# Down projection of a decoder layer: 520 tokens divided into two moving parts, group by group

## The chip, the cores and the metric
The program runs on one NeuronCore of a Trainium2 chip (trn2). The metric is device time in microseconds, from launch to end, as the median of several executions. One further execution is taken with the hardware profiler; its views are what this document reads. TensorE (PE) does the matmuls and loads their weights (PEld), VectorE (DVE), ScalarE (ACT) and GpSimd (POOL) do the elementwise work, and SyncE (SP) issues all DMAs from one queue, in order.

## The reference
One decoder layer over 512 prompt tokens and 8 sample tokens, 520 in all, with a model width of 2048. A mixer (gated spatial heads beside a gated linear recurrence) is followed by a SwiGLU feed-forward net of width 5632, both with RMS norms before and after. What matters here is the end:

```
h = rms_norm(x, g_ffn_pre)
f = (silu(h @ w_gate) * (h @ w_up)) @ w_down
x = x + rms_norm(f, g_ffn_post)
```

`silu(h @ w_gate) * (h @ w_up)` are called the gated rows here: 5632 rows by 520 tokens, in 44 depth tiles of 128 rows.

## The kernel before
Activations lie transposed: features on the 128 partitions, tokens along the free dimension. The 520 tokens (`T`) are cut into two halves of 260 columns (`HT`, `cols(h)`). All large products are done in f32r, a 32-bit type with which a matmul needs one pass, and each operand is split into a high part (a cast to f32r) and a low part (the rest, by a subtraction). A product is the sum of three matmuls: high weights by high rows, high weights by low rows, low weights by high rows. In `product` these are lines 103 to 105; each has 128 x 128 weights as the stationary and 260 columns as the moving operand, and loads its own weights.

Weights come from DRAM as raw tiles of 128 x 1024 (tag `wr`, 3 buffers, line 74), are cast by ScalarE (`wh`, line 82, 4 buffers) and subtracted by VectorE (`wl`, line 84, 4 buffers). `pieces` keeps two pieces fetched beyond the ones in use.

Before the down projection, `seven` computes 40 of the 44 depth tiles of gated rows, in pairs, with seven block products for gate and up each (`term`, lines 736 to 738), and writes them to the DRAM tensor `fd` (line 795). The first four depth tiles were computed before (`gated`) and lie in `fd` too.

The down projection divides the 44 depth tiles into six groups, `CHUNKS = (4, 8, 8, 8, 8, 8)`. For one group the gated rows stand in SBUF as high and low halves: `load_f` reads one depth tile of 128 x 520 from `fd` into a `G` tile (line 789) and splits each half of 260 columns into its own pair of tiles of pool `ap` (`split`, lines 112 and 113; 64 buffers of 260 columns, the pool that also holds the rows of all earlier products). For each of the 16 output tiles `m`, `down` takes one piece of weights and computes the two halves one after the other, each with 3 matmuls per depth tile, 24 in a row (12 in the first group). The result is copied to the accumulator `Y[m]` in the first group (line 809) and added to it in the others (line 811). After every second output tile one depth tile of the next group is loaded and split.

The last group runs with the halves as the outer loop, and its weights are fetched twice. While the second half is computed, `finish_half(0)` normalises the first half, adds the residual rows `x1d` (line 829 loads them into tiles of `ap`, 16 per half) and writes it out (line 858). After the last matmul `finish_half(1)` does the same for the second half, with nine of the sixteen sums made by identity matmuls on TensorE (lines 839 and 851), the rest on VectorE (line 856), and the output of line 860.

Instructions are put in order by the scheduler of the kernel's framework: it takes what is ready in the order of the program, and where a tile has to be waited for, later instructions can be issued ahead of the one that waits. Each engine and the DMA queue then run their instructions strictly in the order so fixed.

The change touches the pools at the head of `trunk`, `load_f`, `down`, the loop that loads the first group, and the tiles of `finish_half`.

Of the kernel before, what the change touches and what calls it, by code (L numbers as in the profile page):

```python
# [7 lines left out]
F32 = mybir.dt.float32  # L8
F32R = mybir.dt.float32r
# [3 lines left out]
ALU = mybir.AluOpType  # L13
PSUM = bass.MemoryType.PSUM

P = 128
NP = 512
NS = 8
T = NP + NS
HT = T // 2  # L20
# [5 lines left out]
EPS = 1e-6  # L26
CHUNKS = (4, 8, 8, 8, 8, 8)
NSK = 4
LEVELS = (32, 8, 2)


@with_exitstack
def trunk(ctx: ExitStack, tc: tile.TileContext, a: dict):
    nc = tc.nc
    vec, act, pe, sp = nc.vector, nc.scalar, nc.tensor, nc.sync

    cp = ctx.enter_context(tc.tile_pool(name="cp", bufs=1))
    wp = ctx.enter_context(tc.tile_pool(name="wp", bufs=4, side="right"))
    ap_ = ctx.enter_context(tc.tile_pool(name="ap", bufs=64))
    phc = ExitStack()  # L40
    cc = phc.enter_context(tc.tile_pool(name="cc", bufs=16, side="right"))
    st = ctx.enter_context(tc.tile_pool(name="st", bufs=2))
    mm = ctx.enter_context(tc.tile_pool(name="mm", bufs=5, space=PSUM))
    ax = ctx.enter_context(tc.tile_pool(name="ax", bufs=3, space=PSUM))

    def const(name, dt=F32):
        t = cp.tile(list(a[name].shape), dt, name=name)
        sp.dma_start(t, a[name])
        return t

    def bank():
        return ax.tile([P, 512], F32, tag="ax", name="ax")

    def cols(h):
        return slice(h * HT, (h + 1) * HT)

    def part(pool, tag, bufs, dt=F32):

        return pool.tile([P, HT], dt, tag=tag, name=tag, bufs=bufs)

    def full(pool, tag, bufs=1, dt=F32):
        return pool.tile([P, T], dt, tag=tag, name=tag, bufs=bufs)
# [27 lines left out]
    def pieces(n, ahead=2):  # L90
        while queue and len(ready) < n + ahead:
            fetch()
        return [ready.pop(0) for _ in range(n)]

    def product(ws, xs, h, place=None):

        ps = place() if place else mm.tile([P, 512], F32, tag="mm", name="mm")
        n = len(xs)
        for k, x in enumerate(xs):
            wh, wl = ws[k // 8]  # L100
            xh, xl = x[h]
            c = slice((k % 8) * P, (k % 8) * P + P)
            pe.matmul(ps[:, :HT], lhsT=wh[:, c], rhs=xh, start=(k == 0), stop=False)  # L103
            pe.matmul(ps[:, :HT], lhsT=wh[:, c], rhs=xl, start=False, stop=False)  # L104
            pe.matmul(ps[:, :HT], lhsT=wl[:, c], rhs=xh, start=False, stop=(k == n - 1))  # L105
        return ps[:, :HT]

    def split(x, pool, tag, bufs, scale=None):
        hi = part(pool, tag, bufs, F32R)
        lo = part(pool, tag, bufs, F32R)  # L110
        if scale is None:
            act.copy(hi, x)
            vec.tensor_tensor(out=lo, in0=x, in1=hi.bitcast(F32), op=ALU.subtract)
        else:
            act.mul(hi, x, scale)
            vec.scalar_tensor_tensor(out=lo, in0=x, scalar=scale, in1=hi.bitcast(F32), op0=ALU.mult, op1=ALU.subtract)
        return hi, lo
# [43 lines left out]
    for i in range(KT):  # L161
# [3 lines left out]
        if i % 4 == 0:  # L165
            c = slice((i % 8) * P, (i % 8 + 4) * P)
# [19 lines left out]
    for k in range(KT):  # L186
        X.append([split(x0[k][:, cols(h)], ap_, "A", 64, g1[:, k:k + 1]) for h in range(2)])
        for m in range(2):
            if k % 8 == 0:
                W[m].append([wp.tile([P, 1024], F32R, tag=t, name=t) for t in ("wh", "wl")])  # L190
            hi, lo = W[m][-1]
            raw = w0[m][k // 8]
            if k % 4 == 0:
                for o, n in ((0, 1), (1, 3)) if k == 0 else ((k % 8, 4),):
                    c = slice(o * P, (o + n) * P)
                    act.copy(hi[:, c], raw[:, c])
                    vec.tensor_tensor(out=lo[:, c], in0=raw[:, c], in1=hi[:, c].bitcast(F32), op=ALU.subtract)
            c = slice((k % 8) * P, (k % 8 + 1) * P)
            for h in range(2):
                ps = first[2 * m + h][:, :HT]  # L200
# [16 lines left out]
    vec.memset(keep.rearrange("p (n t) -> p n t", t=32)[:, :, 0:1], 0.0)  # L217
    masks = {h: const(f"mask{h}", I32) for h in LEVELS[1:]}
    mone = const("mask1", I32)
# [18 lines left out]
    def step():  # L238
        for g in list(behind):
            if next(g, StopIteration) is StopIteration:  # L240
                behind.remove(g)

    ws = pieces(2)
# [303 lines left out]
    for h in range(8):  # L547
        w = {}
# [29 lines left out]
    for _ in range(2):  # L578
        for i in range(NSK):
            for nm in ("w_gate", "w_up"):  # L580
# [12 lines left out]
    fd = tc.dram_tile([FT, P, T], F32, name="fd")  # L593
# [30 lines left out]
    for h in range(2):  # L624
        for m in range(16):
            ps = product(pieces(2), OS, h)
# [29 lines left out]
    def combine():  # L656
        c0, c1 = cols(0), cols(1)
        for k in range(8):
            lo, hi = M[k], M[k + 8]
            vec.tensor_tensor(out=lo[:, c0], in0=lo[:, c1], in1=lo[:, c0], op=ALU.subtract)  # L660
            T1[k] = split(lo[:, c0], tp, "T", 48)
            nc.gpsimd.tensor_tensor(out=lo[:, c1], in0=hi[:, c1], in1=lo[:, c1], op=ALU.subtract)
            vec.tensor_tensor(out=hi[:, c1], in0=hi[:, c1], in1=lo[:, c0], op=ALU.subtract)
            T2[k] = split(hi[:, c1], tp, "T", 48)
            nc.gpsimd.tensor_tensor(out=hi[:, c0], in0=hi[:, c1], in1=hi[:, c0], op=ALU.subtract)
            T3[k] = split(lo[:, c1], tp, "T", 48)
            yield

    for i in range(NSK):
        g = product(pieces(2), X, 0)  # L670
# [8 lines left out]
    behind.append(combine())  # L679
    for i in range(NSK):  # L680
        g = product(pieces(2), X, 1)
        step()
        last = i == NSK - 1
        u = product(pieces(2, 0 if last else 2), X, 1)
# [12 lines left out]
    gp_ = ph4.enter_context(tc.tile_pool(name="gp", bufs=8, side="right", reuse_waits="tile"))  # L697
# [80 lines left out]

    for i in range(NSK, FT, 2):
        for nm in ("w_gate", "w_up"):  # L780
            queue.extend(quarters(a[nm], i, i == NSK and nm == "w_gate"))
    for n in (0, 1, 2, 3, 4, 5, 5):
        for m in range(16):
            want(a["w_down"][n - 1, m] if n else a["w_head"][m], 1024 if n else 512)
    F = []

    def load_f(i):
        f = full(gp_, "G", 8)
        sp.dma_start(f, fd[i])
        return [split(f[:, cols(h)], ap_, "A", 64) for h in range(2)]  # L790

    for i in range(NSK, FT, 2):
        gate = seven(None)
        for j, f in enumerate(seven(gate)):
            sp.dma_start(fd[i + j], f)
    for i in range(CHUNKS[0]):
        F.append(load_f(i))
    ph2.close()


    yp = ctx.enter_context(tc.tile_pool(name="yp", bufs=16, reuse_waits="tile"))
    Y = [None] * 16

    def down(ws, m, h, c):
        ps = product(ws, F, h)
        if Y[m] is None:
            Y[m] = full(yp, "Y", 16)
        if c == 0:
            act.copy(Y[m][:, cols(h)], ps)
        else:  # L810
            vec.tensor_tensor(out=Y[m][:, cols(h)], in0=ps, in1=Y[m][:, cols(h)], op=ALU.add)  # L811

    done = CHUNKS[0]
    for c in range(len(CHUNKS) - 1):
        G = []
        for m in range(16):
            ws = pieces(1)
            for h in range(2):
                down(ws, m, h, c)
            if m % 2:  # L820
                G.append(load_f(done))
                done += 1
        F = G

    def finish_half(h):
        xs = []
        for i in range(16):
            xs.append(part(ap_, "A", 64))
            sp.dma_start(xs[i], x1d[i, h])
        yield  # L830
        with tc.high_priority(4000):
            r = inv_rms(acc[h], D, load=False)

        sums = []

        def add(i):
            ps = bank() if i % 7 in (0, 3) else mm.tile([P, 512], F32, tag="mm", name="mm")
            sums.append(ps[:, :HT])
            pe.matmul(sums[i], lhsT=ident, rhs=xs[i], start=True, stop=False)

        for i in range(7 if h else 0):
            add(i)
        yield
        c = cols(h)
        for i in range(16):
            y = Y[i][:, c]

            o = Y[i & ~1][:, cols(i % 2)] if h else xs[i]
            vec.tensor_tensor(out=y, in0=y, in1=r, op=ALU.mult)
            if i < len(sums):  # L850
                pe.matmul(sums[i], lhsT=ident, rhs=y, start=False, stop=True)
                act.copy(o, sums[i])
                if i + 7 < 9:
                    add(i + 7)
            else:
                vec.tensor_tensor(out=o, in0=y, in1=xs[i], op=ALU.add)
            if h == 0:
                sp.dma_start(a["o_y"][i, h], o)
            elif i % 2:
                sp.dma_start(a["o_y"][i - 1:i + 1, h].rearrange("i p t -> p i t"), Y[i - 1].rearrange("p (i t) -> p i t", i=2))  # L860
            yield
# [4 lines left out]
    for h in range(2):  # L866
        next(ends[h])
        for m in range(16):
            down(pieces(1), m, h, 5)
            y = Y[m][:, cols(h)]  # L870
            add_square(acc[h], y, m == 0)
            act.mul(y, y, gf[:, m:m + 1])
            step()
        while behind:
            step()
        behind.append(ends[h])
# [5 lines left out]
def layouts(x_prompt, x_sample, state_hgrn, norm_mix_pre, norm_mix_post, w_in, ln_v_gain, ln_v_bias, spatial_w,  # L882
# [34 lines left out]
    arrays["ident"] = np.eye(P, dtype=np.float32)  # L917
    for hh in LEVELS[1:]:
        g = 32 // hh
# [38 lines left out]
```

## Time and profile before

| | |
|---|---|
| median of 2 runs | 2323.53 us (2323.21 to 2323.84) |
| profiled execution | 2318.88 us |
| its span, first to last instruction | 2317.2 us |
| mean granted TensorE clock | 0.993 |
| TensorE busy | 2266.3 us, 98% |
| VectorE busy | 1664.3 us, 72% |
| ScalarE busy | 1065.9 us, 46% |
| GpSimd busy | 220.6 us, 10% |
| DMA, mean rate | 134 GB/s |

All times in the views are microseconds from the start of the span, or nanoseconds where it says so. A matmul's duration in the trace includes the time it takes to pass through the array, during which the next one already runs; how fast matmuls follow one another is read from their starts, or from how many start in a stretch. The down projection lies between 1793 and 2300 us.

### The profile page before, as it was taken

The page shows a single profiled execution, that of the slowest core. Times are in us where ns is not written, and L with a number is a line of the kernel's source. Part 1 is how long each engine was busy: PE and PEld are TensorE (multiplying, and loading weights), DVE is VectorE, ACT ScalarE, POOL GpSimd, SP SyncE. Part 2 cuts the span into 40 slices and gives each one's busy share as a digit, 9 for nine tenths or more (in the row PEclk, how much of TensorE's full clock was granted, in tenths as well). Part 3 has the DMA queues.
Part 4 walks back from the last instruction along what each step waited for, and adds up shares of the span by engine and source line. Part 5 has one row for each costly group of instructions (what it writes and reads, how often), then busy time and mean ns, then how long its engine had stood idle before and what let it go on. Part 6 is the DMA issues. An engine that isn't in the chain of part 4 may idle for free.

```text
span 2317.2 us, 44793 instructions
## 1 busy us (share of the span) xinstructions
PE 2266.3 (98%) x18548; PEld 2256.2 (97%) x18548; DVE 1664.3 (72%) x2688; ACT 1065.9 (46%) x1607; POOL 220.6 (10%) x116
## 2 busy tenths in 40 slices
PE   8999999999999998999999999999999999999998
PEld 8999999999999998999999999999999999999998
DVE  8398777777555778888888888888888534434367
ACT  7286566666345555444343443444334512212155
POOL 0000000000000000322222222222221000000000
PEclk9999999999999999999999999999999999999999
DMA  6224333443335766543333333333333723332275
GB/s 224 92 88 125 113 114 111 120 120 120 115 110 182 214 209 194 176 158 115 115 110 126 119 115 124 119 120 110 118 119 102 229 92 129 112 113 95 90 240 156
DMA packets 130267, 310.16 MB, mean 134 GB/s; under 512 B 14928, under 2 KB 57360, under 8 KB 130064
## 3 DMA queue, kind: packets, MB, share of 16 engines
q1 hardware_dynamic: 130064, 307.30, 42.7%
q8 instruction: 145, 2.38, 0.4%
q14 instruction: 58, 0.48, 0.1%
HBM read 281.64 MB, written 25.61 MB: 133 GB/s over the span
## 4 chain that ended last, share of the span: by engine, by line
PE 80%; DVE 9%; DMA 8%; ACT 1%; issue 1%; SPq 0%; DVEq 0%; POOL 0%; ACTq 0%; POOLq 0%
PE mm L105 14%; PE mm L104 14%; PE mm L103 14%; PE mm L738 8%; PE mm L736 8%; PE mm L737 8%; DMA bc<-scr 5%; PE ax L738 3%; PE ax L736 3%; PE ax L737 3%; DVE wl L84 2%; PE ax L411 1%; DMA scr<-rows 1%; DMA wr<-w_up 1%; DVE S L483 1%
## 5 line engine op out<-in xcount | busy, mean ns | idle before, releaser
L105 PE MATMUL mm<-A,wl 128*128 128x260 f32 x3616 | 1026.2, 284 | 8.7 <-DVE wl L84 8.4
L103 PE MATMUL mm<-A,wh 128*128 128x260 f32 x3616 | 1031.3, 285 | 2.0 <-ACT wh L82 2.0
L104 PE MATMUL mm<-A,wh 128*128 128x260 f32 x3616 | 1026.0, 284 | 0.0
L82 ACT CAST wh<-wr 128x1024 fp32r<-128x1024 f32 (+1 forms) x460 | 475.4, 1035 | 771.6 <-PE mm L104 475.4
L84 DVE TENSOR_TENSOR wl<-wr,wh 128x1024 fp32r<-128x1024 f32 (+1 forms) x460 | 554.7, 1207 | 268.4 <-ACT wh L82 255.8
L105 PEld LDWEIGHTS mm<-A,wl 128*128 128x128 f32 x3616 | 685.0, 189 | 10.5 <-DVE wl L84 10.3
L103 PEld LDWEIGHTS mm<-A,wh 128*128 128x128 f32 x3616 | 684.8, 189 | 2.5 <-ACT wh L82 2.2
L104 PEld LDWEIGHTS mm<-A,wh 128*128 128x128 f32 x3616 | 685.0, 189 | 0.3
L738 PE MATMUL mm<-A,wl 128*128 128x260 f32 x960 | 271.1, 282 | 0.5 <-DVE wl L84 0.5
L737 PE MATMUL mm<-A,wh 128*128 128x260 f32 x960 | 270.8, 282 | 0.0
L736 PE MATMUL mm<-A,wh 128*128 128x260 f32 x960 | 270.4, 282 | 0.0
L82 ACT CAST wh<-ws 128x1024 fp32r<-128x1024 f32 x120 | 123.8, 1047 | 265.8 <-DVE ws L719 265.8
L811 DVE TENSOR_TENSOR Y<-mm,Y 128x260 f32<-128x260 f32 x160 | 68.4, 427 | 193.0 <-PE mm L105 192.8
L84 DVE TENSOR_TENSOR wl<-ws,wh 128x1024 fp32r<-128x1024 f32 x120 | 188.4, 1570 | 11.8 <-ACT wh L82 10.8
L736 PE MATMUL mm<-T,wh 128*128 128x260 f32 x640 | 181.4, 283 | 1.3 <-ACT wh L82 1.3
L738 PE MATMUL mm<-T,wl 128*128 128x260 f32 x640 | 180.8, 282 | 0.8 <-DVE wl L84 0.8
L738 PEld LDWEIGHTS mm<-A,wl 128*128 128x128 f32 x960 | 180.2, 188 | 0.7 <-DVE wl L84 0.7
L737 PEld LDWEIGHTS mm<-A,wh 128*128 128x128 f32 x960 | 180.8, 188 | 0.0
L736 PEld LDWEIGHTS mm<-A,wh 128*128 128x128 f32 x960 | 180.7, 188 | 0.0
L737 PE MATMUL mm<-T,wh 128*128 128x260 f32 x640 | 180.1, 281 | 0.0
L720 POOL TENSOR_TENSOR wr<-wr 128x1024 f32<-128x1024 f32 x40 | 95.8, 2396 | 478.5 <-DVE ws L717 478.5
L719 DVE TENSOR_TENSOR ws<-ws,wr 128x1024 f32<-128x1024 f32 x40 | 134.3, 3358 | 0.0
(229 smaller groups left out, 3123.2 us busy)
## 6 DMA issues: line engine op xcount, KB each, us to landing
wr<-w_gate SPq DMA_DIRECT2D x96, 512.0 KB, 4.0
wr<-w_up SPq DMA_DIRECT2D x96, 512.0 KB, 4.1
wr<-w_down SPq DMA_DIRECT2D x96, 512.0 KB, 3.6
wr<-w_in SPq DMA_DIRECT2D x92, 512.0 KB, 4.1
wr<-w_out SPq DMA_DIRECT2D x64, 512.0 KB, 3.8
bc<-scr SPq DMA_DIRECT2D x32, 384.0 KB, 5.3
G<-fd SPq DMA_DIRECT2D x44, 260.0 KB, 3.9
fd<-G SPq DMA_DIRECT2D x40, 260.0 KB, 3.6
```

The costliest lines, as they stand in the source:

```text
L82: act.copy(hi[:, :n], raw[:, :n])
L84: vec.tensor_tensor(out=lo[:, :n], in0=raw[:, :n], in1=hi[:, :n].bitcast(F32), op=ALU.subtract)
L103: pe.matmul(ps[:, :HT], lhsT=wh[:, c], rhs=xh, start=(k == 0), stop=False)
L104: pe.matmul(ps[:, :HT], lhsT=wh[:, c], rhs=xl, start=False, stop=False)
L105: pe.matmul(ps[:, :HT], lhsT=wl[:, c], rhs=xh, start=False, stop=(k == n - 1))
L411: pe.matmul(pl[:, c * 192:(c + 1) * 192], lhsT=kk[:, cg * P:(cg + 1) * P], rhs=qq[:, cg], start=True, stop=True)
L719: vec.tensor_tensor(out=s2, in0=s1, in1=raws["11"], op=ALU.subtract)
L720: nc.gpsimd.tensor_tensor(out=raws["21"], in0=raws["11"], in1=raws["21"], op=ALU.subtract)
L736: pe.matmul(ps, lhsT=wh[:, c], rhs=xh, start=(start and k == 0), stop=False, skip_group_check=not start)
L737: pe.matmul(ps, lhsT=wh[:, c], rhs=xl, start=False, stop=False, skip_group_check=not start)
L738: pe.matmul(ps, lhsT=wl[:, c], rhs=xh, start=False, stop=(k == len(xs) - 1), skip_group_check=not start)
L811: vec.tensor_tensor(out=Y[m][:, cols(h)], in0=ps, in1=Y[m][:, cols(h)], op=ALU.add)
```

## The change
A list `CUTS` gives each group its own division of the 520 tokens: in the six groups the first part has 260, 256, 260, 512, 384 and 260 columns, and the second part the other 260, 264, 260, 8, 136 and 260. `load_f` makes one high and one low tile of 544 columns (2176 bytes) per depth tile, in a pool `fp` of 32 buffers, with one cast and one subtraction over all 520 columns; the parts are slices of these tiles. In the third group the second half is put 12 columns further on, so that it begins at byte 1088 of its tile; elsewhere the second part follows directly on the first. `down` holds the three matmuls itself. The pool `ap` is closed before the down projection, and the residual rows of `finish_half` take tiles of `fp`. The number of matmuls, the weights and their order stay.

```diff
+CUTS = ((260, False), (256, False), (260, True), (512, False), (384, False), (260, False))
...
-    ap_ = ctx.enter_context(tc.tile_pool(name="ap", bufs=64))
+    st = ctx.enter_context(tc.tile_pool(name="st", bufs=2))
+    pha = ExitStack()
+    ap_ = pha.enter_context(tc.tile_pool(name="ap", bufs=64))
...
-    def load_f(i):
-        f = full(gp_, "G", 8)
-        sp.dma_start(f, fd[i])
-        return [split(f[:, cols(h)], ap_, "A", 64) for h in range(2)]
...
-    for i in range(CHUNKS[0]):
-        F.append(load_f(i))
     ph2.close()
+    pha.close()
+    fp = ctx.enter_context(tc.tile_pool(name="fp", bufs=32, reuse_waits="tile"))
...
+    def load_f(i, c):
+        cut, gap = CUTS[c]
+        f = full(gp_, "G", 8)
+        sp.dma_start(f, fd[i])
+        hi, lo = (fp.tile([P, T + 24], F32R, tag="F", name="F", bufs=32) for _ in range(2))
+        if gap:
+            def two(t):
+                return t[:, :T + 24].rearrange("p (h t) -> p h t", h=2)[:, :, :HT]
+            f2 = f.rearrange("p (h t) -> p h t", h=2)
+            act.copy(two(hi), f2)
+            vec.tensor_tensor(out=two(lo), in0=f2, in1=two(hi).bitcast(F32), op=ALU.subtract)
+            return [(hi[:, o:o + HT], lo[:, o:o + HT]) for o in (0, HT + 12)]
+        act.copy(hi[:, :T], f)
+        vec.tensor_tensor(out=lo[:, :T], in0=f, in1=hi[:, :T].bitcast(F32), op=ALU.subtract)
+        return [(hi[:, x], lo[:, x]) for x in (slice(0, cut), slice(cut, T))]
+
     def down(ws, m, h, c):
-        ps = product(ws, F, h)
+        cut, gap = CUTS[c]
+        x = (slice(0, cut), slice(cut, T))[h]
+        (wh, wl), = ws
+        ps = mm.tile([P, 512], F32, tag="mm", name="mm")[:, :x.stop - x.start]
+        for k, f in enumerate(F):
+            fh, fl = f[h]
+            w = slice(k * P, k * P + P)
+            pe.matmul(ps, lhsT=wh[:, w], rhs=fh, start=(k == 0), stop=False)
+            pe.matmul(ps, lhsT=wh[:, w], rhs=fl, start=False, stop=False)
+            pe.matmul(ps, lhsT=wl[:, w], rhs=fh, start=False, stop=(k == len(F) - 1))
         if Y[m] is None:
             Y[m] = full(yp, "Y", 16)
         if c == 0:
-            act.copy(Y[m][:, cols(h)], ps)
+            act.copy(Y[m][:, x], ps)
         else:
-            vec.tensor_tensor(out=Y[m][:, cols(h)], in0=ps, in1=Y[m][:, cols(h)], op=ALU.add)
+            vec.tensor_tensor(out=Y[m][:, x], in0=ps, in1=Y[m][:, x], op=ALU.add)
+    for i in range(CHUNKS[0]):
+        F.append(load_f(i, 0))
...
-                G.append(load_f(done))
+                G.append(load_f(done, c + 1))
...
-            xs.append(part(ap_, "A", 64))
+            xs.append(part(fp, "F", 32))
```

## Rows read from the trace of the kernel before

**Rows 1.** The page's head, busy shares and chain that ended last.
```profile
PE 2266.3 (98%) x18548; PEld 2256.2 (97%) x18548; DVE 1664.3 (72%) x2688; ACT 1065.9 (46%) x1607; POOL 220.6 (10%) x116
PE 80%; DVE 9%; DMA 8%; ACT 1%; issue 1%; SPq 0%; DVEq 0%; POOL 0%; ACTq 0%; POOLq 0%
```

**Rows 2.** Stretches of the down projection: busy time (instructions) by engine, clock, DMA.
```profile
1932.00:2022.00 90.00, 90.00 (x757) 90.00 (x756) 37.15 (x61) 21.59 (x32) 0.00 (x0) 1.00 0.35 111
2024.00:2114.00 90.00, 90.00 (x752) 90.00 (x751) 36.63 (x59) 21.21 (x32) 0.00 (x0) 1.00 0.36 110
2208.00:2300.00 92.00, 92.00 (x769) 91.74 (x768) 69.53 (x126) 56.95 (x93) 0.00 (x0) 1.00 0.68 212
```

**Rows 3.** A stretch at half clock, then TensorE's order of time around it.
```profile
439.90:443.20 3.30, 2.74 (x13) 2.77 (x14) 3.30 (x7) 2.00 (x4) 0.00 (x0) 0.50 0.34 100
...
440.46 1.09 PE L437 MATMUL ax<-ident,kh 128*128 128x128 f32 x4 [2.65 <-DVE kh L357]
...
441.77 0.42 PE L105 MATMUL mm<-A,wl 128*128 128x260 f32 x1
441.99 0.42 PE L103 MATMUL mm<-A,wh 128*128 128x260 f32 x1
```

**Rows 4.** Order of time in the first group: matmuls and weight loads.
```profile
1800.07 0.19 PEld L103 LDWEIGHTS mm<-A,wh 128*128 128x128 f32 x1
1800.19 0.29 PE L103 MATMUL mm<-A,wh 128*128 128x260 f32 x1
1800.19 0.19 PEld L104 LDWEIGHTS mm<-A,wh 128*128 128x128 f32 x1
```

**Rows 5.** Order of time: f32 matmuls of 128 columns, four and two in a row.
```profile
186.55 0.61 PE L518 MATMUL ax<-A,ibt 128*128 128x128 f32 x4
...
186.99 0.39 PE L520 MATMUL ax<-qh,Sc 128*128 128x128 f32 x2
```

**Rows 6.** f32 matmuls of 192 columns: eight in a row, and their group's mean.
```profile
143.78 1.46 PE L411 MATMUL ax<-qx,kx 128*128 128x192 f32 x8
...
L411 PE MATMUL ax<-qx,kx 128*128 128x192 f32 x192 | 36.0, 329 | 0.0
```

**Rows 7.** Groups by line (busy us, mean ns): splits of 260 columns, and operations of 520.
```profile
L112 ACT CAST A<-G 128x260 fp32r<-128x260 f32 x88 | 29.9, 407 | 3.3 <-DMA G<-fd 3.2
L113 DVE TENSOR_TENSOR A<-G,A 128x260 fp32r<-128x260 f32 x88 | 32.5, 422 | 3.2 <-ACT A L112 3.0
L774 ACT ACTIVATE G<-G 128x520 f32<-128x520 f32 x20 | 12.8, 640 | 7.3 <-DVE G L772 7.3
L179 DVE TENSOR_TENSOR C<-C 128x520 f32<-128x520 f32 x15 | 10.5, 702 | 0.7
```

**Rows 8.** Order of time at the stage's start: ScalarE, then VectorE.
```profile
1794.55 1.53 ACT L112 CAST A<-G 128x260 fp32r<-128x260 f32 x4 [0.37 <-DMA G<-fd]
...
1795.61 1.44 DVE L113 TENSOR_TENSOR A<-G,A 128x260 fp32r<-128x260 f32 x4
```

**Rows 9.** SP's order of time at the end, its waits, landings.
```profile
2230.65 0.38 SPq L829 DMA_DIRECT2D A<-x1d  x1
2262.55 0.82 SPq L858 DMA_DIRECT2D o_y<-A  x2
2283.66 8.49 SPq L858 DMA_DIRECT2D o_y<-A  x5
...
SPq L477 <- DMA o_ss<-S: 34.8, 18, 3.7
...
A<-x1d SPq DMA_DIRECT2D x32, 130.0 KB, 3.5
o_y<-A SPq DMA_DIRECT2D x16, 130.0 KB, 4.5
```

**Rows 10.** Order of time at the end: first and last use of the rows.
```profile
2300.18 1.92 PE L839 MATMUL mm<-A,ident 128*128 128x260 f32 x8
2312.92 0.43 DVE L856 TENSOR_TENSOR Y<-Y,A 128x260 f32<-128x260 f32 x1
```

More of the change, by code (lines that the diff above doesn't have):

```diff
@@ L38, in trunk @@
     wp = ctx.enter_context(tc.tile_pool(name="wp", bufs=4, side="right"))
-    ap_ = ctx.enter_context(tc.tile_pool(name="ap", bufs=64))
+    st = ctx.enter_context(tc.tile_pool(name="st", bufs=2))
+    pha = ExitStack()
+    ap_ = pha.enter_context(tc.tile_pool(name="ap", bufs=64))
     phc = ExitStack()
     cc = phc.enter_context(tc.tile_pool(name="cc", bufs=16, side="right"))
-    st = ctx.enter_context(tc.tile_pool(name="st", bufs=2))
     mm = ctx.enter_context(tc.tile_pool(name="mm", bufs=5, space=PSUM))
```

## The prediction
> **What bounds the kernel now.** I read the page from its top: the busy shares, then the chain of work that ended last [rows 1]. TensorE is busy for 98% of the span and the chain lies on it for 80%. I cut the time of the down projection into stretches, each inside one group of depth tiles; three of them stand here [rows 2]. In all of them TensorE is busy for the whole stretch at full clock, while VectorE is busy for some 40% and ScalarE for 24%, more only in the last one, where the norms and outputs come in. So this stage is bound by how often a matmul can start: 752 in 90 us are 119.7 ns from start to start, 757 are 118.9, and I use 120. The 260 columns of one matmul would take 108.3 ns at 2.4 GHz; where the clock stands at half (1.2 GHz) they start 0.22 us apart, which is 260/1.2 = 217 ns with nothing added [rows 3]. At full clock there are thus 11.7 ns more than the columns explain.
>
> The order of time inside the stage [rows 4] shows what else each matmul needs: a weight load of its own. The load for the next matmul starts when the present one starts, and the next one follows 0.12 us later. That a load is never earlier is the row on which this prediction hangs. How fast loads can follow each other when the columns are few is seen at the f32 matmuls of 128 columns [rows 5]: four in 0.61 us, two in 0.39, so (0.61 - 0.39)/2 = 110 ns apart, and I take 111. (An f32 matmul runs two cycles a column, 107 ns here, so the load alone could be shorter; that is rival (a).)
>
> **The change, part by part.** Each group keeps its number of matmuls: 16 output tiles by 8 depth tiles by 3 products by 2 parts, which is 384 pairs (192 in the first group, with 4 depth tiles). A pair now costs 240 ns. Only the columns of the two halves of a pair change, and `down` runs all 24 matmuls of one part before the other, so a short part cannot hide its loads behind a long one.
>
> Fourth group, 512 and 8. The long one: 512/2.4 = 213.3 ns, plus the 11.7 of the 260 as a fixed addition, 225. Ends: 215, if almost nothing is added (the f32 matmuls of 192 columns [rows 6] take 0.329 us each and eight of them 1.46, so they start (1.46 - 0.33)/7 = 161 ns apart, little over the 160 of two cycles a column), and 236, if the addition grows with the columns (120 x 512/260). The short one streams 8 columns in 3 ns but loads 128 columns of weights: 111, ends 109 and 120 (what a load and matmul take today). Sum 336 (324 to 356), 96 more per pair, and 384 x 96 = **36.9 us** (32 to 45). No row has loads closer together than that, so I take the load as the bound. The Trainium skill ("TensorE: Matmul & The Clock Gate", section "Back-to-back issue gap") speaks against this: N/2.4 + 2.5 ns, with a floor of some 60 cycles. By it the pair would be 215.8 + 25 = 241 ns and the group would cost nothing; this stands below as a rival.
>
> Fifth group, 384 and 136. 160 + 11.7 = 172 (162 to 177), and for 136, whose columns need only 57 ns, again the load, 111 (109 to 120): 283 (271 to 297), 43 more, 384 x 43 = **16.4 us** (12 to 22).
>
> Second group, 256 and 264: 118.4 + 121.7 = 240 with the fixed addition, the same in proportion: **0**. If 256 falls to the load's 111 it is 384 x -7 = -3 us.
>
> First, third and last group, 260 and 260. The second half now begins 1040 bytes into its tile, in the third group 1088. No row shows a half that shares a tile. The stretches of [rows 2] differ by 0.8 ns though their tiles lie at other places; half of that for 1,920 matmuls is 1 us either way, and I take **0**.
>
> The split of the gated rows. Per tile two casts and two subtractions of 260 columns (407 and 422 ns) become one of each with 520, which cost about what the 520-column operations of the trace cost, 640 and 702 [rows 7]. That saves some 0.3 us a tile on both engines, under cover of TensorE: a tile is loaded per two output tiles, at least 2 x 24 x 120 ns = 5.8 us apart. The cover is missing only at the start of the stage. There the casts of the third and fourth tile begin at 1794.55 and their subtractions run to 1797, with matmuls already waiting for them tile by tile [rows 8]; both halves must now be split before the first part can use them: 2 x (702 - 422) + (640 - 407) = 0.8 us. The tile memory is no later: the new tiles lie over those that the last but one `term` of `seven` frees. I take **1 us**; ends 0 (the wait falls into slack) and 4 (all four tiles are split after that stage's last matmul: 4 x 0.70 + 0.64, and the DMA behind).
>
> The end. `finish_half` took its residual rows from 64 half tiles, both halves early: the last of the 32 loads is issued at 2231, before the first output of line 858 at 2262 [rows 9]. Now 32 full tiles hold the last group's 16 and the first half's 16 rows, so each row of the second half must wait until the output DMA of a first-half row has left its tile; those outputs go out between 2262 and 2292. SP issues in order, and behind such a wait stand the weight loads of the last group, for which the casts and then TensorE wait. The same pattern, a DMA into a tile that a DMA must leave, is there at line 477: 34.8 us in 18 waits, 1.9 each, at most 3.7. Sixteen of them are 31 us within the last 38 us of matmuls, beside 27 weight and output issues of 0.33: SP is nearly full, but weights are fetched two to three pieces ahead and one piece lasts 24 x 120 ns = 2.9 us. The last rows would land around 2292 + 4.5 + 3.5 = 2300, and they are first used at 2300 to 2313 [rows 10]. I take **2 us**, ends 0 and 10 (half of what 16 waits of 3.7 would exceed the 38 us by). A gain is excluded: nothing is taken off the path there.
>
> Sum: 36.9 + 16.4 + 0 + 0 + 1 + 2 = **56 us** (low 32 + 12 - 3 - 1 = 40, high 45 + 22 + 1 + 4 + 10 = 82). The profiled execution took 2318.9 us for a span of 2317.2, and so 2375 with the change; the median of the runs, 2323.5, lies 4.6 above it, so I forecast 2380 (2364 to 2405).
>
> **Rivals.**
> (a) *Columns alone set the pace.* If loads are pulled further ahead when matmuls are short, a pair costs 520 columns however they are divided: 120/260 x 520 = 240 ns in every group, and only the 3 us of the split and the end are left, 2327: no change. It decides if 8-column matmuls start much closer than 109 ns. For it speaks that the 260 columns are not bound by the load alone, which could go at 110; against it that in no row does a load start before the preceding matmul has started. By the skill's gap rule named above, 256 and 384 would even gain (222 ns for each of these pairs), and the time would be about 2313.
> (b) *The clock falls in the fourth group.* Each run of 24 short matmuls lasts 24 x 111 = 2.7 us and streams 192 columns in it. With a wait of TensorE of 2.65 us, the clock came to stand at half from 439.9 to 443.2 [rows 3]. If TensorE counts as idle in such a run, each fall costs a stretch of 3.3 us in which 260 columns take 0.217 instead of 0.12, so about 1.5 us; with 16 runs, 24 us: 2404. If the clock stays down for the group, a pair costs 427 + 222, 313 more, and it is 2500. Against it: the loads go on throughout.
> (c) *Few columns lose the fast f32r rate.* All f32r matmuls of the trace have 260 columns. The f32 ones of 192 columns stand in the trace as two records of 161 ns [rows 6], 1.68 ns a column. If 136 columns run so, they take 229 instead of 111, 384 x 118 = 45 us more: 2425; if 8 columns too load their weights twice, another 43: 2468. The trace neither shows nor excludes it.
> (d) *The end of the kernel* is SP's: if each of the 16 waits lasts the 4.5 us of such an output's median landing [rows 9], they are 72 us, 34 more than the 38: 2380 - 2 + 34 = 2412.
>
> **How the numbers follow.** Forecast 0.48, (a) 0.12, (b) 0.17, (c) 0.17, (d) 0.04, and 0.02 for a gain that I cannot place. The predicted time is the forecast's, 2380. The range leaves out (a), the worse half of (c) and the rare end of (b): 2358 to 2435. The 2% that a measurement of this kernel can tell from no change are 46 us, a bound at 2370. All of (b), (c), (d) lie above it, and of the forecast's 2364 to 2405 about five parts in six: slower 0.78. Within 2%: (a) and the rest of the forecast, 0.20. Faster by over 2% would need all 4,224 matmuls 11 ns shorter, which no row suggests: 0.02.
>
> **What would show it.** In the profile after, matmuls of 8 and of 136 columns start 109 to 120 ns apart, those of 512 and 384 some 225 and 172; the fourth group lasts about 129 us, the fifth 109, the others 92 (46 for the first). Starts at 4 to 60 ns prove (a), half clock in the fourth group (b), 200 ns and more at 136 columns (c), and idle TensorE in the last 46 us behind SP (d). The forecast is wrong if the short parts come cheaper than a load, or if the columns over 260 cost more than in proportion.

## The result and the profile after

The changed kernel takes 2402.35 us (median of 2 runs, 2398.49 to 2406.21) against 2323.53: ratio 1.034, 95% interval 1.027 to 1.041. It is slower by 79 us, where 57 were forecast as the likeliest and 35 to 112 as the range. Its profiled execution took 2406.21 us for a span of 2404.5, 87.3 more than the span before.

Where these 87.3 us lie is read by cutting the down projection at the first matmul of each group, in both traces (us from the first start of a group to the first of the next; group 6 ends at the first matmul of the sums behind it):

| stretch | before | after | more | forecast |
|---|---|---|---|---|
| up to the last matmul of `seven` | 1793.0 | 1799.4 | 6.4 | 0 |
| from there to the stage's first matmul | 0.1 | 1.4 | 1.3 | 1 |
| group 1, 260 and 260 | 46.5 | 46.6 | 0.1 | 0 |
| group 2, 256 and 264 | 92.1 | 92.4 | 0.3 | 0 |
| group 3, 260 and 260 with the gap | 91.6 | 92.5 | 0.9 | 0 |
| group 4, 512 and 8 | 92.2 | 149.2 | **57.0** | 36.9 |
| group 5, 384 and 136 | 92.3 | 111.7 | **19.4** | 16.4 |
| group 6, 260 and 260 | 92.4 | 93.9 | 1.5 | 2 with the end |
| from that matmul to the end | 17.0 | 17.4 | 0.4 | |

The first row is not the change: it varies by 16 us between executions of kernels that are the same up to there (the last section). Without it the table gives 81 us, close to the 79 of the medians.

The stretches of groups 2, 4, 5 and 6 in the changed kernel, to be held against [rows 2]; columns as there, the first of the last three is TensorE's granted clock:

```profile
1848.00:1938.00 90.00, 90.00 (x751) 90.00 (x750) 34.48 (x51) 18.32 (x21) 0.00 (x0) 1.00 0.34 108
2032.20:2181.40 149.20, 149.20 (x770) 127.55 (x768) 36.65 (x54) 19.18 (x21) 0.00 (x0) 0.87 0.23 71
2181.50:2293.10 111.60, 111.60 (x769) 111.60 (x769) 38.09 (x56) 21.81 (x24) 0.00 (x0) 0.98 0.26 78
2293.20:2387.00 93.80, 93.80 (x772) 93.59 (x772) 69.99 (x126) 57.14 (x93) 0.00 (x0) 1.00 0.72 212
```

TensorE is busy throughout, as before, and the same 768 matmuls stand in each of the last three stretches. What changed is how far apart they start, and in the fourth group the clock: 0.87 on average. The clock's own record has twelve stretches of 3.41 us at half behind that group's sixteen runs of short matmuls, against none in the same groups before. Eleven lie in group 4; the twelfth begins 0.9 us into group 5, behind the last run.

One turn from short to long matmuls in that group, in order of time:

```profile
2058.27 0.25 PE L827 MATMUL mm<-F,wh 128*128 128x8 f32 x1
2058.38 0.25 PE L828 MATMUL mm<-F,wl 128*128 128x8 f32 x1
2058.49 0.47 PE L826 MATMUL mm<-F,wh 128*128 128x512 f32 x1
2058.80 0.39 PE L827 MATMUL mm<-F,wh 128*128 128x512 f32 x1
2059.03 0.40 PE L828 MATMUL mm<-F,wl 128*128 128x512 f32 x1
2059.27 0.41 PE L826 MATMUL mm<-F,wh 128*128 128x512 f32 x1
2059.50 0.60 PE L827 MATMUL mm<-F,wh 128*128 128x512 f32 x1
2059.90 0.63 PE L828 MATMUL mm<-F,wl 128*128 128x512 f32 x1
2060.32 0.63 PE L826 MATMUL mm<-F,wh 128*128 128x512 f32 x1
...
2062.88 0.42 PE L826 MATMUL mm<-F,wh 128*128 128x512 f32 x1
2063.14 0.40 PE L827 MATMUL mm<-F,wh 128*128 128x512 f32 x1
2063.38 0.40 PE L828 MATMUL mm<-F,wl 128*128 128x512 f32 x1
```

Matmuls of 8 columns start 0.11 us apart: the weight load, as forecast. Those of 512 start 0.23 apart until 2059.50 (the first of a run 0.31), then some 0.43, and from 2062.88 on 0.23 to 0.26 again. The median at half clock, 427 ns, is 512/1.2: the clock is at half for 3.4 us, right behind a run of short matmuls. The two stretches at the two levels of the clock:

```profile
2059.50:2062.90 3.40, 3.40 (x10) 2.62 (x9) 1.23 (x1) 0.11 (x1) 0.00 (x0) 0.50 0.29 52
2062.90:2065.60 2.70, 2.70 (x13) 2.21 (x12) 0.00 (x0) 0.00 (x0) 0.00 (x0) 0.99 0.32 129
```

Rival (b) thus stands beside the forecast, not in its place. The price in group 4: eleven times 3.41 us in which a 512-column matmul takes 427 ns instead of 234, so 11 x 3.41 x (1 - 234/427) = 17.0 us. In group 5 the twelfth makes matmuls of 384 columns take 320 ns instead of 175: 3.41 x (1 - 175/320) = 1.5 us. Together they are 18.5 us. Four of the sixteen runs have no fall behind them; no run shows why.

### The profile page after: what moved, and what is told of

Its sections match the earlier page's. It is cut to its first block, busy times and chain, and to the rows that moved or that the text cites. A ratio compares the mean times of both kernels' runs of the same rounds, so it can differ in the third digit from the quotient of the medians.

```text
span 2404.5 us, 44695 instructions
## 1 busy us (share of the span) xinstructions
PE 2345.1 (98%) x18548; PEld 2313.1 (96%) x18548; DVE 1661.6 (69%) x2644; ACT 1061.7 (44%) x1563; POOL 221.3 (9%) x116
## 4 chain that ended last, share of the span: by engine, by line
PE 82%; DMA 8%; DVE 7%; ACT 1%; issue 1%; SPq 0%; DVEq 0%; POOL 0%; ACTq 0%; POOLq 0%
PE mm L828 8%; PE mm L826 8%; PE mm L827 8%; PE mm L739 8%; PE mm L741 8%; PE mm L740 8%; PE mm L107 7%; PE mm L106 7%; PE mm L108 7%; DMA bc<-scr 5%; PE ax L740 3%; PE ax L739 3%; PE ax L741 3%; DVE wl L87 1%; PE ax L414 1%
## 5 line engine op out<-in xcount | busy, mean ns | idle before, releaser
L108 PE MATMUL mm<-A,wl 128*128 128x260 f32 x2208 | 630.3, 286 | 9.6 <-DVE wl L87 9.5
L106 PE MATMUL mm<-A,wh 128*128 128x260 f32 x2208 | 637.5, 289 | 2.0 <-ACT wh L85 1.9
L107 PE MATMUL mm<-A,wh 128*128 128x260 f32 x2208 | 631.0, 286 | 0.0
L108 PEld LDWEIGHTS mm<-A,wl 128*128 128x128 f32 x2208 | 422.5, 191 | 11.3 <-DVE wl L87 11.1
L106 PEld LDWEIGHTS mm<-A,wh 128*128 128x128 f32 x2208 | 424.3, 192 | 2.8 <-ACT wh L85 2.4
L107 PEld LDWEIGHTS mm<-A,wh 128*128 128x128 f32 x2208 | 423.1, 192 | 0.2
L826 PE MATMUL mm<-F,wh 128*128 128x260 f32 (+6 forms) x1408 | 422.0, 300 | 1.1 <-ACT F L814 1.1
L827 PE MATMUL mm<-F,wh 128*128 128x260 f32 (+6 forms) x1408 | 422.3, 300 | 0.0
L828 PE MATMUL mm<-F,wl 128*128 128x260 f32 (+6 forms) x1408 | 422.0, 300 | 0.0
L826 PEld LDWEIGHTS mm<-F,wh 128*128 128x128 f32 x1408 | 270.3, 192 | 8.6 <-ACT F L814 1.3
L827 PEld LDWEIGHTS mm<-F,wh 128*128 128x128 f32 x1408 | 270.9, 192 | 7.3
L828 PEld LDWEIGHTS mm<-F,wl 128*128 128x128 f32 x1408 | 270.6, 192 | 7.3
L741 PE MATMUL mm<-A,wl 128*128 128x260 f32 x960 | 270.2, 282 | 0.4 <-DVE wl L87 0.4
L740 PE MATMUL mm<-A,wh 128*128 128x260 f32 x960 | 270.5, 282 | 0.0
L739 PE MATMUL mm<-A,wh 128*128 128x260 f32 x960 | 270.5, 282 | 0.0
L834 DVE TENSOR_TENSOR Y<-mm,Y 128x260 f32<-128x260 f32 (+6 forms) x160 | 68.5, 428 | 263.6 <-PE mm L828 263.6
L739 PE MATMUL mm<-T,wh 128*128 128x260 f32 x640 | 181.4, 283 | 1.6 <-ACT wh L85 1.6
```

The source lines that it names most:

```text
L739: pe.matmul(ps, lhsT=wh[:, c], rhs=xh, start=(start and k == 0), stop=False, skip_group_check=not start)
L740: pe.matmul(ps, lhsT=wh[:, c], rhs=xl, start=False, stop=False, skip_group_check=not start)
L741: pe.matmul(ps, lhsT=wl[:, c], rhs=xh, start=False, stop=(k == len(xs) - 1), skip_group_check=not start)
L826: pe.matmul(ps, lhsT=wh[:, w], rhs=fh, start=(k == 0), stop=False)
L827: pe.matmul(ps, lhsT=wh[:, w], rhs=fl, start=False, stop=False)
L828: pe.matmul(ps, lhsT=wl[:, w], rhs=fh, start=False, stop=(k == len(F) - 1))
```

## The experiments

The theory: a matmul costs the longer of its weight load (111 ns for 128 columns of weights) and its columns, and a run of 24 matmuls with hardly any columns makes the clock fall. The rivals: matmuls of 512 columns are slow in themselves; short f32r matmuls run at the f32 rate; the split, the pools and SP at the end cost more than the division. All kernels below are the changed kernel with other entries in `CUTS`, plus what is shown. Runs 5, 6, 7, 9 and 10 are one execution each and are read by their groups.

**1. 260 everywhere.** The new split and pools alone.

```diff
-CUTS = ((260, False), (256, False), (260, True), (512, False), (384, False), (260, False))
+CUTS = ((260, False), (260, False), (260, False), (260, False), (260, False), (260, False))
```


> The changed kernel with 260 and 260 columns in all six groups, second half directly behind the first. If the cost is in the division alone, every group is back at 92 to 93 us (46 the first) and the time is 2324 to 2330: the 1.3 us at the start of the stage and under 2 us at its end stay. If the split for all tokens, the pools or the residual rows cost more (rival), it is above 2335.

Measured: 2325.11 us against 2322.67 for the kernel before on the same chip, ratio 1.001 (0.9997 to 1.0022). The groups last 46.5, 93.2, 92.6, 92.3, 92.8 and 93.9 us. So the division of groups 4 and 5 is nearly the whole of the loss; split, pools and end cost 2 us by these times, if anything. In the two traces the stage is longer by more, 6.0 us from the last matmul of `seven` to the end: 1.3 at its start, 4.3 in the groups and 0.4 behind them.

**2. 512 and 8 alone.** As 1, with 512 in the fourth group.

> As the run with 260 everywhere, but 512 and 8 in the fourth group. Forecast plus falls of the clock: the fourth group lasts 149 us, so 57 more than with halves, about 2382; matmuls of 8 columns 111 ns apart, those of 512 some 234 at full clock and 427 at half. Forecast alone (load of 111 beside 225 to 236 per pair, clock full): 129 to 134 us, 2362 to 2367.

Measured: 2380.24 us, ratio 1.0257 (1.0240 to 1.0275). The fourth group takes 150.8 us, 58.5 more than in run 1, with twelve stretches at half clock; every other group is within 0.1 us of run 1.

**3. 384 and 136 alone.** As 1, with 384 in the fifth group.

> As the run with 260 everywhere, but 384 and 136 in the fifth group. Load as the bound of the short part: 111 + 176 per pair, the group 110 to 112 us, 18 to 19 more than with halves, about 2345, with no more half clock in the group than the 3.4 us that the group inherited in the changed kernel. Short parts at the f32 rate (rival c): 229 ns at 136 columns, the group 155 us.

Measured: 2338.80 us, ratio 1.0077 (1.0062 to 1.0092). The time is 6 us under what was expected, the group itself at the bottom of it: 110.1 us, 17.3 more than in run 1. Matmuls of 136 columns start 110 to 112 ns apart and those of 384 some 175, and the clock stays full:

```profile
2113.50:2223.40 109.90, 109.90 (x769) 109.90 (x768) 36.34 (x54) 19.88 (x21) 0.00 (x0) 1.00 0.26 80
```

The 1.6 us that group 5 has more in the changed kernel (clock 0.98 there) are the twelfth fall, 1.5 us. The f32 rate at 136 columns, rival (c), is refuted.

**4. Long and short in turn.** As 2, but in the fourth group each product's two matmuls follow one another.

```diff
...
+        for k, f in enumerate(F):
+            w = slice(k * P, k * P + P)
+            for j, (wt, e) in enumerate(((wh, 0), (wh, 1), (wl, 0))):
+                for h in range(2):
+                    pe.matmul(ps[h], lhsT=wt[:, w], rhs=f[h][e], start=(k == 0 and j == 0), stop=(k == n and j == 2))
...
```


> 512 and 8 in the fourth group as before, the same 768 matmuls and loads, but the long and the short matmul of each product alternate instead of standing in runs of 24. If the clock falls because a run of short matmuls leaves TensorE nearly idle, it stays full here, and the group lasts 384 x (234 + 111) = 132 us, 17 less than with the runs: about 2366. If the half clock comes from the matmuls of 512 columns, or if short matmuls cost more than a load in themselves, the group stays at 149 us and 2382.

Measured: 2363.64 us, ratio 1.0179 (1.0164 to 1.0194), 16.6 less than run 2. The group, in the same view as above, here and then in run 2:

```profile
2025.90:2157.20 131.30, 131.30 (x770) 114.71 (x769) 38.72 (x60) 23.05 (x28) 0.00 (x0) 1.00 0.25 81
```
```profile
2020.10:2170.80 150.70, 150.70 (x769) 128.66 (x768) 36.54 (x54) 19.13 (x21) 0.00 (x0) 0.86 0.22 70
```

The same matmuls and loads take 131.3 us at full clock and 150.7 with runs. The runs of short matmuls bring the clock down; that costs 19 us, and the twelve falls, all inside this group in run 2, are worth 18.5 by the price above. The remaining 39 us over run 1's 92.3 are the load: a pair costs 342 ns. Its starts are 316 ns (long to short) and 26 ns (short to long) apart, and the loads go one matmul ahead, as in [rows 4]: the short one's begins beside the long matmul, the long one's only 2 to 3 ns after the start of the short one.

```profile
2080.22 0.48 PE L846 MATMUL mm<-F,wh 128*128 128x512 f32 x1
2080.30 0.19 PEld L846 LDWEIGHTS mm<-F,wh 128*128 128x128 f32 x1
...
2080.54 0.19 PEld L846 LDWEIGHTS mm<-F,wh 128*128 128x128 f32 x1
```

Two loads of 111 ns would fit beside the 234 ns of the long matmul. Only one stands there, and the other has 8 columns to hide behind.

**5. Runs of 48.** As 2, but two output tiles together: 48 long matmuls, then 48 short ones.

```diff
-            ws = pieces(1)
-            for h in range(2):
-                down(ws, m, h, c)
+            if c != 3:
+                ws = pieces(1)
+                for h in range(2):
+                    down(ws, m, h, c)
+            elif m % 2 == 0:
+                two = [pieces(1), pieces(1)]
+                for h in range(2):
+                    for e in range(2):
+                        down(two[e], m + e, h, c)
```


> 512 and 8 in the fourth group, but two output tiles together: 48 long matmuls, then 48 short ones, so runs of 5.3 us with almost no columns, half as many of them. If the clock falls because of the runs, half clock takes a larger share of the group than the 41 us of twelve falls, and the group lasts longer than 150 us. If each fall belongs to a change between long and short matmuls, there are at most eight, and it lasts about 141 us.

Measured: 2387.84 us; the group lasts 152.7 us at a mean clock of 0.85. There are eight stretches at half clock of 3.4 to 10.2 us each, as many as short runs. Seven lie in the group, 44 us, and the eighth begins with the next one. Six of them begin while short matmuls still run, 2.2 to 5.0 us after the first of their run:

```profile
2043.63 0.25 PE L827 MATMUL mm<-F,wh 128*128 128x8 f32 x1
2043.74 0.25 PE L828 MATMUL mm<-F,wl 128*128 128x8 f32 x1
2043.85 0.29 PE L826 MATMUL mm<-F,wh 128*128 128x8 f32 x1
2044.01 0.36 PE L827 MATMUL mm<-F,wh 128*128 128x8 f32 x1
2044.22 0.35 PE L828 MATMUL mm<-F,wl 128*128 128x8 f32 x1
2044.43 0.77 PE L826 MATMUL mm<-F,wh 128*128 128x512 f32 x1
```

So the fall belongs to the run of short matmuls, not to the turn to long ones, and half as many turns do not halve the loss. That the group is longer than with runs of 24 holds by 2 us only.

**6. Six other divisions.** `CUTS` with 496, 448, 416, 352, 320 and 288 columns first.

> Six divisions in one kernel: 496 and 24 (the first group), 448 and 72, 416 and 104, 352 and 168, 320 and 200, 288 and 232. If a short part costs its load, all of them start 108 to 112 ns apart, whatever their columns, and the long ones follow 2.9 + 0.45 N: 226, 205, 190, 161, 147, 133 ns. Groups at full clock: 65, 121, 116, 105, 99 and 94 us, 88 more than with halves, about 2413, and more where the clock falls. With the addition fixed at 11.7 ns (the forecast's middle) the long ones are 218, 198, 185, 158, 145, 132. If short parts ran at the f32 rate of 1.68 ns a column, 104 columns and more would cost 175 to 390 ns.

Measured: 2419.11 us. The groups, in the same view:

```profile
1784.90:1849.70 64.80, 64.80 (x384) 57.44 (x384) 22.88 (x33) 29.48 (x62) 0.00 (x0) 1.00 0.54 172
1849.80:1971.00 121.20, 121.20 (x770) 115.16 (x769) 37.16 (x54) 20.68 (x26) 0.00 (x0) 1.00 0.26 82
1971.10:2086.80 115.70, 115.70 (x769) 114.74 (x769) 37.94 (x57) 20.85 (x25) 0.00 (x0) 1.00 0.29 92
2086.90:2191.60 104.70, 104.70 (x770) 104.70 (x769) 37.86 (x57) 20.99 (x25) 0.00 (x0) 1.00 0.32 102
2191.70:2290.60 98.90, 98.90 (x769) 98.90 (x769) 36.43 (x54) 20.02 (x21) 0.00 (x0) 1.00 0.28 87
2290.70:2400.30 109.60, 99.74 (x771) 98.74 (x771) 70.45 (x126) 57.29 (x93) 0.00 (x0) 0.95 0.58 183
```

Five groups are where they were expected, within 0.3 us. The median distance from one matmul's start to the next of the same width, over the 192 or 384 of each width (8, 136, 256 and 264 from the changed kernel, 260 from run 1, 384 from run 3, 512 from run 7, where the clock stayed full; 232 where it was full):

| columns | 8 | 24 | 72 | 104 | 136 | 168 | 200 | 232 |
|---|---|---|---|---|---|---|---|---|
| ns | 112 | 112 | 112 | 111 | 112 | 111 | 111 | 113 |

| columns | 256 | 260 | 264 | 288 | 320 | 352 | 384 | 416 | 448 | 496 | 512 |
|---|---|---|---|---|---|---|---|---|---|---|---|
| ns | 118 | 120 | 121 | 133 | 146 | 161 | 175 | 190 | 206 | 226 | 234 |

Up to 232 columns the load sets 111 to 113 ns, whatever the columns; above that 3 + 0.45 N holds within 2 ns. The clock stayed full with 24 columns in runs of 12 and with 72 columns in runs of 24. The last group alone missed: 109.6 us instead of 94, with TensorE idle for 9.9 us (run 9).

**7. Half the weights.** 512 and 8, and 384 and 136, where the matmuls of 8 and of 384 columns load 64 columns of weights. The kernel leaves out half the output rows of these parts.

```diff
+        q = 64 if (c, h) in ((3, 1), (4, 0)) else P
...
-            w = slice(k * P, k * P + P)
+            w = slice(k * P, k * P + q)
...
```


> 512 and 8 in the fourth group, 384 and 136 in the fifth; the matmuls of 8 and those of 384 columns use 64 columns of weights instead of 128, so half the output rows of these parts are left out. If 8 columns cost the load, they start 55 to 60 ns apart instead of 111; if it is a fixed time of a matmul with few columns, 111 stays. If the 8% over 2.4 columns per ns of the long ones come from the load running beside them, 384 falls from 176 to about 168 ns; if they belong to the f32r columns themselves, 176 stays.

Measured: 2360.64 us; matmuls of 8 columns start 58 ns apart, of 384 columns 174.4 on average, against 177.1 in run 3 (medians 174 and 175). The rows of one turn, and the two groups:

```profile
2039.85 0.20 PE L827 MATMUL mm<-F,wh 128*64 128x8 f32 x1
2039.91 0.20 PE L828 MATMUL mm<-F,wh 128*64 128x8 f32 x1
2039.97 0.20 PE L829 MATMUL mm<-F,wl 128*64 128x8 f32 x1
```
```profile
2026.00:2138.50 112.50, 112.50 (x770) 94.47 (x768) 36.51 (x54) 19.20 (x21) 0.00 (x0) 1.00 0.30 94
2138.50:2247.50 109.00, 109.00 (x772) 94.36 (x770) 37.76 (x56) 21.74 (x24) 0.00 (x0) 1.00 0.26 80
```

The 111 ns are the load, shown: half the weights, half the time. The 0.45 ns per column are nearly all the columns' own: 384/2.4 are 160 ns, and of the 17 above that, on average, the halved load took away 3. With runs of 24 x 58 ns = 1.4 us the clock stayed full, so here too the fourth group has no fall.

**8. The gap everywhere.** As 1, with `True` in all six entries.

> 260 and 260 in all six groups, the second half 12 columns further on in its tile, so that it begins at a multiple of 64 bytes. If the place of the second half matters, every group is shorter than in the run without the gap (93.2, 92.6, 92.3, 92.8 and 93.9 us), by 1 us or more each, and the time some 5 us less; if not, the time is within 2 us of that run, 2325.

Measured: 2322.42 us, ratio 1.0001 (0.9987 to 1.0014); groups of 46.5, 92.4, 92.5, 92.4, 92.6 and 92.8 us. The second and the last are 0.9 and 1.1 us shorter than in run 1, the others within 0.2: 2 us in all, which the times cannot tell apart from run 1. The expectation of 5 us is missed.

**9 to 11. The end.** Run 9 is run 1 with 288 and 232 in the last group. Run 10 gives the second half's residual rows tiles of their own as well. Run 11 has the gap everywhere and these tiles.

```diff
+    xq = ctx.enter_context(tc.tile_pool(name="xq", bufs=16, reuse_waits="tile"))
...
-            xs.append(part(fp, "F", 32))
+            xs.append(part(xq, "X", 16) if h else part(fp, "F", 32))
```


> 260 and 260 in five groups, 288 and 232 in the last one, where the second half's residual rows wait for the first half's outputs on SP. In the run of six divisions TensorE waited there for weights, 8 us and more, and the clock fell. If that belongs to the last group itself, this kernel has the same: the last group lasts 105 to 110 us. If it came from the five unequal groups ahead, 94 us.

> The same, but the second half's 16 residual rows have tiles of their own and wait for no output. If SP's waits for the outputs are what holds the weights back, the last group lasts about 384 x (133 + 111) = 94 us, TensorE waits under 1 us in it, and no load of these rows waits for an output. If the weights are late for another reason (the order on the queue, or the rate of the loads), TensorE still waits 8 us.

> 260 and 260 with the gap in all six groups, and tiles of their own for the second half's residual rows: the split for all tokens without its cost at the end. If that cost is SP's, the last group falls from 92.8 to 92.4 us and the time is that of the kernel before, 2322 within 2 us; no gain over it is expected.

Measured: run 9 takes 2342.94 us, its last group 112.0; run 10 2331.03 and 103.3; run 11 2322.32, ratio 0.9998 (0.9986 to 1.0010), and 92.8. Who waited for whom on TensorE and on SP from 2205 us on (total us, times, longest), run 9, then run 10:

```profile
PE mm L826 <- ACT wh L85: 5.0, 2, 3.8
PE mm L828 <- DVE wl L87: 3.6, 3, 2.3
...
SPq L854 <- DMA o_y<-F: 8.8, 8, 3.7
```
```profile
PE mm L829 <- DVE wl L87: 4.0, 1, 4.0
...
SPq L77 <- DVE acc L148: 59.8, 23, 3.1
```

In run 9 the weights come late and SP waits for outputs; with own tiles those waits are gone, and TensorE still waits 4 us, where under 1 or 8 was expected. In the last group the clock stands at half for 13.7 us in run 9 and for 6.8 us in run 10, which is part of what they lose. So rival (d) exists, but only with this division: the order on the queue changes, and in run 10 nine outputs in 5.55 us stand ahead of the next weight load:

```profile
2272.90 0.34 SPq L77 DMA_DIRECT2D wr<-w_down  x1
2273.91 5.55 SPq L884 DMA_DIRECT2D o_y<-F  x9
2280.58 15.89 SPq L77 DMA_DIRECT2D wr<-w_down  x8
```

That this order holds up the rest is read from the queue, not tested. With halves in the last group (run 8 against run 11, 92.8 both, where 92.4 was expected) the waits cost nothing. No version came out faster than the kernel before.

## Why the prediction was right, point by point

**The short part costs its load:** right in mechanism and size, 111 to 112 ns for 8 and 136 columns. Run 7 shows that it is the load. Rival (a) is refuted by run 4 too, where both loads of a pair would have fitted beside its 512 columns, and the pair still cost 342 ns. So it is not the runs of 24 that keep a short part from hiding its loads, as the prediction has it: a load goes one matmul ahead and no further. By the gap rule of the Trainium skill ("TensorE: Matmul & The Clock Gate", section "Back-to-back issue gap") the estimate would have been 25 ns there and 216 at 512 columns, and the group at no loss; the runs measured 111 and 234. The section gives that rule for a matmul by itself and says that in a stream with weight loads both set the spacing, so it does not speak against the load as the prediction took it to. The Trainium skill (the same page, section "LDWEIGHTS (loading the stationary operand)") gives the load P/1.2 ns for P columns, an estimate of 107 and 53 ns for 128 and 64 columns; the starts were 111 and 58 ns apart, at full clock, which agrees within 5 ns.

**The long part:** the addition to the columns was put as fixed, 225 ns at 512. It grows with the columns: 234, close to the end of 236 that the forecast kept. The term was too small by 9 ns, or 384 x 9 = 3.5 us, and by 3 ns x 384 = 1.2 us for 384 columns.

**The clock:** the forecast held it full and gave rival (b) 0.17. This is the term that failed: "the loads go on throughout" was no reason against a fall. Priced at sixteen falls of 1.5 us, 24 us, it measured twelve, 18.5 us. With it and the long part, group 4 becomes 36.9 + 3.5 + 17.0 = 57.4 against 57.0 measured, and group 5 16.4 + 1.2 + 1.5 = 19.1 against 19.4. The measured 2402 is thus what rival (b) gave, 2404; that it also lies below the forecast's own upper end, 2405, is luck, since that end stood for dearer loads, columns and waits at a full clock.

**256 and 264, and the second half behind the first:** 0 was forecast; 0.3 and 0.9 us in groups 2 and 3, and of the 1.5 in the last one 1.1 go away with the gap (run 8). The 1 us either way was about right here; without any gap (run 1) the six groups have 4.3 us more than before.

**The start of the stage:** 1 us forecast, 1.3 measured, but not by the working given. The working took it that the new tiles come no later; the trace shows their casts later. The casts begin after the last matmul of `seven`, on ScalarE right behind a weight cast that had waited 2.22 us for TensorE, and TensorE waits for the first of them:

```profile
1799.43 0.28 PE L741 MATMUL ax<-A,wl 128*128 128x260 f32 x1
1799.63 0.62 ACT L85 CAST wh<-wr 128x512 fp32r<-128x512 f32 x1 [2.22 <-PE ax L740]
1800.15 2.21 ACT L814 CAST F<-G 128x520 fp32r<-128x520 f32 x4
1800.83 0.87 PE L826 MATMUL mm<-F,wh 128*128 128x260 f32 x5 [1.12 <-ACT F L814]
```

Before, the first casts were done while that product ran, and only the later ones waited, for their DMA [rows 8]. Whether the tiles' memory or only the order on ScalarE put the casts so late, no run separates.

**The end:** 2 us were forecast for SP's waits. They are there, 14.2 us in 11 instead of 31 in 16, and no matmul of the last group waits behind them:

```profile
SPq L854 <- DMA o_y<-F: 14.2, 11, 2.7
```

**Order on the queues** was taken as it stood; run 9 shows that a shorter last part would have made rival (d) true.

## What to carry to other kernels

Where every matmul loads its own weights, a moving part of fewer than about 240 columns costs as much as one of 240 here ((111 - 3)/0.45), so 520 columns belong in two nearly equal parts; a division with a shorter part pays the full load for it. Ask of a short part not only what it costs but what the clock does behind a run of such parts: putting long and short matmuls in turn gave back 19 of 58 us without taking away one instruction. Take a fixed addition and a proportional one both through the sum when a size leaves the range that the trace shows.

## What the runs showed of the hardware beyond that

Columns of f32r flow at 0.45 ns each at full clock, from 256 to 512 columns, not at the 0.417 of 2.4 GHz; at half clock they take 1/1.2 ns (427 for 512, 320 for 384). Half the load beside them changes little of it, and why it is so stays open. The load slows with the clock: matmuls of 8 columns start 213 ns apart at half clock (run 5) and 112 at full clock.

The part before the down projection is the same program in all kernels with the changed pools, and yet its last matmul starts anywhere from 1783.5 (run 6) to 1799.4 us (the changed kernel). Nearly all of the difference is the clock: up to 1790 us it stands at half for 47.8 us in the changed kernel and for 17.1 in run 6, and the 30.7 us between them cost 15.4 us against full clock. It lies in the mixer part, where TensorE often waits. The stretch from 180 to 1010 us in the changed kernel, then in run 6:

```profile
180.00:1010.00 830.00, 787.18 (x6281) 780.34 (x6281) 604.23 (x1351) 459.34 (x717) 31.32 (x31) 0.97 0.48 143
```
```profile
180.00:1010.00 830.00, 791.63 (x6416) 784.57 (x6416) 616.68 (x1363) 466.77 (x726) 37.44 (x33) 0.99 0.48 146
```

135 matmuls fewer at 0.97 than at 0.99 are 16 us at 120 ns. One profile against another is therefore read stage by stage; their totals differ by that much for no reason of the change.
